# A chunked delta-rule recurrence: products with the same shape of stationary tile issued directly together

## The chip, the core and the metric

The kernel runs on one core of a Trainium2 chip. The metric is the device time in microseconds (us) of one execution. TensorE (PE in the profile) does matrix products, VectorE (DVE) and ScalarE (ACT) elementwise work, GpSimd (POOL) a few powers and fills, and the SyncE queue (SP) issues the transfers.

## The reference, cut to what matters

Two layers of a decoder trunk on 256 tokens of width 2048, float32. Layer 0 runs an RG-LRU and an mLSTM side by side. Layer 1, where the change lies, is an RWKV-7 time mixing: 64 heads of 64 features, and for each head a state matrix that is updated token by token.

```python
def step(S, inp):
    r_t, w_t, k_t, v_t, kk_t, a_t = inp
    sa = jnp.einsum('bhvk,bhk->bhv', S, -kk_t)
    S = (S * w_t[:, :, None, :] + sa[..., None] * (kk_t * a_t)[:, :, None, :]
         + v_t[..., None] * k_t[:, :, None, :])
    return S, jnp.einsum('bhvk,bhk->bhv', S, r_t)
...
u = h @ w_in                       # 2048 x 16384: r, k, v and the gate z
...
y = head_norm(y.reshape(B, S, RWKV_WIDTH), H, RWKV_GN_EPS, gn_g, gn_b)
bonus = jnp.sum(rh * kh * r_k.astype(jnp.float32), axis=-1, keepdims=True) * vh
...
return (y * jax.nn.silu(z)) @ w_out
```

## The kernel before, in words

Most of the time goes to four big projections (in and out of each layer). Their weights are loaded in pieces (`raw`), and each piece is split into a high part (`whi`, copied by ACT) and the rest (`wlo`, subtracted by DVE), so that three products replace one float32 product: `hh` and `hl` (high part and rest of the activations) with `whi`, then `hh` with `wlo`. These products write banks named `gb`. A piece of an input projection is 16 products with `whi` and 8 with `wlo`.

Everything else (the mixers) writes banks named `mb` and is woven between those products. A mixer is a Python generator; a `yield w` says how much projection work should come before its next step. `Weave` counts the projection work as it is written out (`tick`, 0.44 for four products) and lets a generator go on when its due time has come; after a step that issued TensorE work it lets at least 0.4 pass. TensorE runs strictly in the order in which it was written (`InOrder`). On DVE and ACT the framework orders the instructions itself, except that none passes a split of the weights that was written before it (`Behind`); the order is fixed when the program is built.

Layer 1 works through eight groups of eight heads (`g` = 0 to 7). A group needs four input projections of 512 columns (k, r, z, v). The recurrence of group g, `recur`, starts when its v is there, and so runs between the products of the k projection of group g+1 (for g = 7 between those of the output projection). It goes over four chunks of 64 tokens. For each chunk `c` there are up to five sets of eight small products (four pairs of heads, two heads each); the letters are used below:

- W: `mb<-UV,At`, all chunks; ACT copies the result to `Ws`;
- U: `mb<-Ws,TT`, all chunks; DVE multiplies the result by `Gn` into `UV`, one half of the partitions at a time;
- S: `mb<-UV,BKt`, chunks 0 to 2, the new state; DVE adds the old state and multiplies by the decay (`Sn<-Sn,mb`, then `Sn<-Sn,PC`), and ACT copies the result in two halves to the next chunk's `UV` (`UV<-Sn`), which the next W reads;
- A: `mb<-UV,At` again, all chunks, the outputs from the current chunk, into the banks `Yb`;
- R: `mb<-Sn,Rc`, chunks 1 to 3, the outputs from the old state, into the same banks.

S and A have stationary tiles of 128 rows by 64 columns; U and R of 64 by 64. Each set stands by itself between projection products. After chunk 1 and after chunk 3 `norm` takes the two banks `Yb`: three copies `Yn<-mb` and a square on ACT, a sum over each head on DVE (`TENSOR_REDUCE vr`), a small `TENSOR_SCALAR vr`, a power on POOL (`vr<-vr,mhalf`), and the product `Yn<-Yn,vr` on DVE, which waits for that power.

At the same time `keys` of group g+1 runs in another lane: when the k projection ends, `kt` and `sq` are made, TensorE sums squares (`mb<-cs,sq`), DVE reads the sums (four `Gn<-mb`), multiplies `kP<-kt,th`, and then makes the eight parts of `BK` from `xx` and `zz`, which ACT makes.

Of the kernel before, what the change touches and what calls it, by code (L numbers as in the profile page):

```python
# [13 lines left out]
P = 128  # L14
# [12 lines left out]
# columns of the packed per-feature vectors: (name, tiles)  # L27
# [18 lines left out]
# columns of the constant array  # L46
# [10 lines left out]
class Weave:  # L57
    """Steps of the mixers, emitted between the products of the projections. A step yields the amount of
    products that come before its lane goes on."""
# [41 lines left out]
class InOrder:  # L101
    """The tensor engine, issuing in the order of the program."""
# [19 lines left out]
class Behind:  # L122
    """An engine whose instructions follow, in its own order, the splits of the weights emitted before them."""
# [20 lines left out]
def two_layers(ctx, tc, x, gpost, cst, selc, v0, v1, w_in0, w_out0, w_in1, w_out1, lruw, qkvw,  # L144
# [36 lines left out]
    def keep_warm(n, b):  # L181
        """Products that keep the clock of the tensor engine up while it waits; nothing reads them."""
        for _ in range(n):
            pe.matmul(b, lhsT=ones[:, 0:P], rhs=ones, start=True, stop=True)
# [15 lines left out]
    # ---------------------------------------------------------------- products  # L200
    def split_w(raw, w=512, into=None):
        """Weights to their high part and the rest."""
# [17 lines left out]
    def in_mms(banks, hi, lo, pc, h, nft, tick):  # L220
        """One piece (two k-tiles) of an input projection: first what needs the high parts of the weights alone."""
# [17 lines left out]
    def in_proj(wsrc, h):  # L239
        """512 columns of an input projection, features on partitions: two banks of two tiles."""  # L240
        banks = [gbank(), gbank()]
        for pc in range(8):
            in_mms(banks, *split_w(load_w(wsrc[pc])), pc, h, 4, 0.44)
        return banks
# [10 lines left out]
    def out_proj(wsrc, get_y, evac, tick, finish, after, room=None):  # L255
        """Output projection, tokens on partitions; get_y(g): the two parts of k-tiles 4g..4g+3. The last
        pieces of the last chunk go token tile by token tile, so that what follows the first is covered."""
# [49 lines left out]
    # ---------------------------------------------------------------- norms, tokens on partitions  # L307
    def rstd(ss):
        """ss [P, 4]: partial sums of squares of a token tile -> [P, 1]."""
# [10 lines left out]
    def scale(ss, pool_):  # L320
        """diag(rstd) of a token tile: transposes by products with it are scaled."""
# [4 lines left out]
    def to_features(xs, dg, g, warm):  # L326
        """Four tiles [P, 2, 512] of tokens, scaled by dg and g, to the two parts of h."""
        banks = {}
# [34 lines left out]
    def log1p_of(e, tmp):  # L363
        """log(1 + e), 0 <= e <= 1, as 2 atanh(e / (2 + e)); tmp: three tiles like e."""
# [12 lines left out]
    def silu2(banks, sz):  # L377
        """sz = 2 silu of two banks."""
# [6 lines left out]
    def residual(layer, tile_of):  # L385
        """The evacuation of out_proj: sums of squares, and the products with the post-norm's weights."""
# [17 lines left out]
    # ================================================================ layer 0  # L404
    with ExitStack() as l0:
# [35 lines left out]
        # small tables  # L441
# [37 lines left out]
        # ------------------------------------------------------------ mLSTM inputs  # L479
# [6 lines left out]
        def mlstm_in(c, xm):  # L486
# [43 lines left out]
            # both gates: two column tiles side by side, summed at the end  # L530
# [104 lines left out]
        # ------------------------------------------------------------ RG-LRU  # L635
# [70 lines left out]
        def room():  # L706
            """Parts of the weights in the place of what the heads have done with."""
# [18 lines left out]
    # ================================================================ layer 1  # L726
    with ExitStack() as l1:
# [19 lines left out]
        # derived per-feature vectors; the halves of the heads' partitions swap B and K  # L747
# [19 lines left out]
        def loras():  # L767
            """The first halves of the two loras: the token shift is taken after the product."""
# [35 lines left out]
        def decay(g, st):  # L804
            """What depends on the loras: the decay within chunks of 64 tokens, and the rate."""
# [481 lines left out]
```

## Time and profile before

| | |
|---|---|
| median of 3 runs | 1917.44 us (1916.8 to 1917.52) |
| profiled execution: span from the first to the last instruction | 1912.7 us |
| median less span: what lies around the span | 4.7 us |
| mean granted TensorE clock | 0.997 |
| PE busy, share of the span | 98% |
| DVE busy | 73% |
| ACT busy | 55% |

Busy times are of instructions from start to end; TensorE's instructions overlap, so that the step from one start to the next is what one costs, and not its duration. A line of the groups or of the timeline gives the engine, the line of the code, the operation, what it writes and reads, the shape, and its time. All matmuls of the kernel have line L116 and all DVE and ACT instructions L132, since helpers record them, so names of tiles tell them apart. A float32 product of the mixers leaves two records in the trace (x16 for a set of eight), a projection product one.

### The profile page before, as it was taken

To read this page: it belongs to the slowest core of one execution; us is meant where nothing else is said; L and a number is where in the kernel's file an instruction comes from. 1 tells how busy PE (TensorE), PEld (TensorE's weight loads), DVE (VectorE), ACT (ScalarE), POOL (GpSimd) and SP (SyncE) were. 2 spreads that over 40 slices of the span, in tenths; PEclk is the share of its full clock that TensorE was granted. 3 is DMA by queue.
4 is the path that set the end of the run, shared out by engine and by line. 5 is a ranking of instruction groups with operands and counts; after the bars stand their busy time and mean duration, and the time that the engine had idled before them with its cause. 6 is when DMAs were issued, how large, how long until landed. Compare 5 with 4: busy or idle time off the path is not lost.

```text
span 1912.7 us, 39517 instructions
## 1 busy us (share of the span) xinstructions
PE 1883.4 (98%) x16498; PEld 1747.9 (91%) x16498; DVE 1395.3 (73%) x2302; ACT 1044.1 (55%) x1609; POOL 60.4 (3%) x84
## 2 busy tenths in 40 slices
PE   8999999999999999999999999999999999999998
PEld 7999999999888899989999999999999999997886
DVE  5667777757554569969689689597796896895544
ACT  5444666645444546555565555655655655555442
POOL 0000000000000100000000000000000000000000
PEclk9999999999999999999999999999999999999999
DMA  7433545455666444434444434344344443356664
GB/s 250 142 133 111 177 162 169 155 171 194 215 208 195 168 147 135 152 118 144 133 136 138 133 130 155 111 147 149 113 150 139 136 136 131 122 187 203 211 202 156
DMA packets 86947, 299.63 MB, mean 157 GB/s; under 512 B 9576, under 2 KB 12392, under 8 KB 86768
## 3 DMA queue, kind: packets, MB, share of 16 engines
q1 hardware_dynamic: 86768, 297.11, 47.2%
q8 instruction: 129, 2.11, 0.5%
q14 instruction: 50, 0.41, 0.1%
HBM read 289.20 MB, written 7.86 MB: 155 GB/s over the span
## 4 chain that ended last, share of the span: by engine, by line
PE 93%; DVE 4%; ACT 1%; issue 1%; DMA 0%; POOL 0%; SPq 0%; DVEq 0%; POOLq 0%; ACTq 0%
PE gb L116 75%; PE mb L116 17%; DVE wlo L132 2%; PE mb L119 1%; DVE wb L132 1%; ACT whi L132 1%; DMA xq<-in_x_dram 0%; DVE rt L132 0%; DVE Tb L132 0%; DVE tf L132 0%; DVE Ab L132 0%; DVE yT L132 0%; ACT ZT L132 0%; ACT vt L132 0%; DVE At L132 0%
## 5 line engine op out<-in xcount | busy, mean ns | idle before, releaser
L132 DVE TENSOR_TENSOR wlo<-raw,whi 128x1024 fp32r<-128x1024 f32 x509 | 619.9, 1219 | 338.0 <-ACT whi L132 304.5
L132 ACT CAST whi<-raw 128x1024 fp32r<-128x1024 f32 x509 | 532.6, 1048 | 557.3 <-PE gb L116 512.3
L116 PE MATMUL gb<-hh,whi 128*128 128x256 f32 x3120 | 790.5, 289 | 2.8 <-ACT whi L132 2.8
L116 PE MATMUL gb<-hl,whi 128*128 128x256 f32 x3120 | 770.6, 283 | 0.0
L116 PEld LDWEIGHTS gb<-hh,whi 128*128 128x128 f32 x3120 | 596.7, 191 | 13.6 <-ACT whi L132 3.7
L116 PEld LDWEIGHTS gb<-hl,whi 128*128 128x128 f32 x3120 | 597.5, 192 | 0.8
L116 PE MATMUL gb<-hh,wlo 128*128 128x256 f32 x3120 | 453.5, 286 | 0.0
L116 PEld LDWEIGHTS gb<-hh,wlo 128*128 128x128 f32 x3120 | 404.9, 191 | 4.2 <-issue 0.7
L116 PE MATMUL gb<-whi,yl 128*128 128x512 f32 x500 | 136.9, 392 | 0.5 <-DVE yl L132 0.5
L116 PE MATMUL gb<-whi,yh 128*128 128x512 f32 x500 | 136.5, 392 | 0.0
L116 PE MATMUL gb<-wlo,yh 128*128 128x512 f32 x500 | 135.7, 390 | 0.0
L116 PEld LDWEIGHTS gb<-whi,yl 128*128 128x128 f32 x500 | 93.2, 188 | 20.4 <-DVE yl L132 0.9
L116 PEld LDWEIGHTS gb<-wlo,yh 128*128 128x128 f32 x500 | 93.5, 188 | 19.8
L116 PEld LDWEIGHTS gb<-whi,yh 128*128 128x128 f32 x500 | 93.0, 188 | 19.3
L132 DVE TENSOR_TENSOR Tb<-Tb,tf 64x31 f32<-64x31 f32 (+15 forms) x248 | 82.6, 333 | 6.1
L132 DVE TENSOR_TENSOR tf<-Ab,Tb 64x31 f32<-64x31 f32 (+15 forms) x248 | 81.9, 330 | 4.5
L116 PE MATMUL mb<-AR,BK 64*128 64x128 f32 (+1 forms) x1024 | 58.0, 253 | 7.0 <-DVE AR L132 6.0
L116 PEld LDWEIGHTS mb<-AR,BK 64*128 64x128 f32 (+1 forms) x1024 | 50.2, 161 | 13.3 <-PE gb L116 7.1
L132 DVE TENSOR_TENSOR UV<-mb,Gn 64x256 f32<-64x256 f32 x64 | 26.9, 421 | 34.5 <-PE mb L116 33.4
L132 ACT ACTIVATE zz<-kP,dv 128x256 f32<-128x256 f32 x64 | 32.3, 505 | 22.9 <-DVE kP L132 12.4
L116 PEld LDWEIGHTS mb<-UV,At 128*64 128x64 f32 (+1 forms) x1024 | 35.0, 137 | 10.3 <-issue 2.5
L1125 POOL TENSOR_TENSOR vr<-vr,mhalf 128x8 f32<-128x8 f32 x16 | 28.3, 1771 | 499.4 <-DVE vr L132 499.4
(258 smaller groups left out, 1855.9 us busy)
## 6 DMA issues: line engine op xcount, KB each, us to landing
raw<-in_w_in_dram SPq DMA_DIRECT2D x384, 512.0 KB, 3.3
raw<-in_w_out_dram SPq DMA_DIRECT2D x128, 512.0 KB, 4.3
y1d<-zt SPq DMA_DIRECT2D x7, 512.0 KB, 3.9
yraw<-y1d SPq DMA_DIRECT2D x7, 512.0 KB, 4.3
l<-in_lora_dram SPq DMA_DIRECT2D x8, 384.0 KB, 4.6
xq<-in_x_dram SPq DMA_DIRECT2D x8, 256.0 KB, 5.2
lw<-in_lruw_dram SPq DMA_DIRECT2D x4, 512.0 KB, 4.6
xr<-in_x_dram SPq DMA_DIRECT2D x8, 256.0 KB, 6.0
```

What stands on the lines that cost most here:

```text
L116: return self._chain(self.eng.matmul(*a, **k))
L119: return self._chain(self.eng.transpose(**k))
L132: r = op(*a, **k)
L1125: pool.tensor_tensor(vr, vr, mhalf[:, 0:8], ALU.pow)
```

## The change

In `recur`, R moves up from the end of its chunk to directly behind U of the same chunk, and opens the accumulation in `Yb`; A moves up to directly behind S and ends it. The two banks `Yb` of chunks 0 and 2 are therefore taken before S and not after it. The two `yield`s behind A and R (0.2 and 0.25) are gone, so that the next chunk's W is due 2.4 after S. The step in which chunk 1 hands its banks to `norm` now comes after that 2.4. Nothing is computed differently, apart from the order of the two terms in the sum. (Comments are gone too; they shift nothing.)

```diff
                 ub = mbank()
...
+                if c % 2 == 0:
+                    Yb = [mbank(), mbank()]
+                cr = [slice(64 * ((c + hd) % 2), 64 * ((c + hd) % 2) + 64) for hd in range(2)]
+                if c:
+                    for f in range(4):
+                        for hd in range(2):
+                            hr = slice(64 * hd, 64 * hd + 64)
+                            pe.matmul(Yb[hd][cr[hd], f * 64:(f + 1) * 64], lhsT=Rc[hr, f, c, :],
+                                      rhs=St[hr, f, :], start=(f == 0), stop=False, skip_group_check=True)
                 for hd in range(2):
                     hr = slice(64 * hd, 64 * hd + 64)
                     dve.tensor_tensor(UV[hr, c, :, hd, :], ub[hr, 0:256].rearrange("p (f v) -> p f v", f=4),
                                       Gn[hr, :, c:c + 1].broadcast_to([64, 4, 64]), MUL)
                 yield 1.8
-                Sp = St
                 if c < 3:
                     sb = mbank()
...
+
+                for f in range(4):
+                    for hd in range(2):
+                        pe.matmul(Yb[hd][cr[hd], f * 64:(f + 1) * 64], lhsT=At[:, f, hd, c, 64:128],
+                                  rhs=UV[:, c, f, hd, :], start=(c == 0 and f == 0),
+                                  stop=True, skip_group_check=True)
+                if c < 3:
                     Sn = g1.tile([P, 4, 64], F32, name="Sn", tag="Sn", bufs=2)
...
                     St = Sn
                     yield 2.4
-                # outputs of this chunk
-                if c % 2 == 0:
-                    Yb = [mbank(), mbank()]
-                cr = [slice(64 * ((c + hd) % 2), 64 * ((c + hd) % 2) + 64) for hd in range(2)]
-                for f in range(4):
-                    for hd in range(2):
-                        pe.matmul(Yb[hd][cr[hd], f * 64:(f + 1) * 64], lhsT=At[:, f, hd, c, 64:128],
-                                  rhs=UV[:, c, f, hd, :], start=(f == 0),
-                                  stop=(c == 0), skip_group_check=True)
-                yield 0.2
-                if c:
-                    for f in range(4):
-                        for hd in range(2):
-                            hr = slice(64 * hd, 64 * hd + 64)
-                            pe.matmul(Yb[hd][cr[hd], f * 64:(f + 1) * 64], lhsT=Rc[hr, f, c, :],
-                                      rhs=Sp[hr, f, :], start=False, stop=True, skip_group_check=True)
-                    yield 0.25
                 if c == 1:
                     nm = wv_.add(norm(0, Yb, Yn, Yn[:, 1]), 2)
```

On TensorE, in chunk 2 of group 3's recurrence, the end of the chunk read as follows before: A, R, and the W of chunk 3, each between projection products.

```order
L116 MATMUL mb<-UV,At 64x64 x8
L116 MATMUL gb<-hh,wlo 128x256 x4
L116 MATMUL mb<-Sn,Rc 64x64 x8
L116 MATMUL gb<-hh,wlo 128x256 x4
L116 MATMUL mb<-UV,At 64x64 x8
```

After the change, U and R of the same chunk stand together, then four projection products and the sums of squares of the next group's keys.

```order
L116 MATMUL gb<-hh,wlo 128x256 x4
L116 MATMUL mb<-Ws,TT 64x64 x8
L116 MATMUL mb<-Sn,Rc 64x64 x8
L116 MATMUL gb<-hh,wlo 128x256 x4
L116 MATMUL mb<-cs,sq 128x2 x8
```

Twelve projection products later S and A stand together, and the W of chunk 3 follows 20 projection products behind them; before, from S to that W, there were 24 projection products, A, 4, R, and 4 more. Over the whole program the stretches of mixer products between projection products go from 307 to 259. The sums of squares stood between the W and the U of chunk 2 before, 16 projection products and U ahead of S; now U and R are past, and 12 projection products lie between the sums and S.

On DVE, the same place read as follows before, from the reading of the sums to the product with the power (names in brackets are the engines waited for):

```order
L132 TENSOR_SCALAR Gn<-mb 64x8 x3
L132 TENSOR_TENSOR kP<-kt,th 128x1024
L132 RECIPROCAL Gn<-Gn 128x16 [waits DVE_49]
L132 TENSOR_TENSOR UV<-mb,Gn 64x4x64 [waits PE_49]
L132 TENSOR_TENSOR UV<-mb,Gn 64x4x64
L132 TENSOR_TENSOR BK<-xx,zz 128x4x64 [waits Activation_49]
L132 TENSOR_REDUCE vr<-Yn 128x8
L132 TENSOR_TENSOR Sn<-Sn,mb 128x256 [waits PE_49]
L132 TENSOR_SCALAR vr<-vr 128x8 [waits DVE_49]
L132 TENSOR_TENSOR Sn<-Sn,PC 128x256 [waits DVE_49]
L132 TENSOR_TENSOR wlo<-raw,whi 128x1024 [waits DMAHW1_49,PE_49,Activation_49]
```

And as follows after the change, in groups 1 to 6 alike:

```order
L132 TENSOR_SCALAR Gn<-mb 64x8 x3
L132 TENSOR_TENSOR kP<-kt,th 128x1024
L132 RECIPROCAL Gn<-Gn 128x16 [waits DVE_49]
L132 TENSOR_REDUCE vr<-Yn 128x8
L132 TENSOR_TENSOR BK<-xx,zz 128x4x64 [waits Activation_49]
L132 TENSOR_SCALAR vr<-vr 128x8 [waits DVE_49]
L132 TENSOR_TENSOR Sn<-Sn,mb 128x256 [waits PE_49]
L132 TENSOR_TENSOR Yn<-Yn,vr 128x512 [waits Pool_49]
L132 TENSOR_TENSOR wlo<-raw,whi 128x1024 [waits DMAHW1_49,PE_49,Activation_49]
L132 TENSOR_TENSOR BK<-xx,zz 128x4x64 [waits Activation_49]
L132 TENSOR_TENSOR Sn<-Sn,PC 128x256 [waits DVE_49]
```

The second product of the state (`Sn<-Sn,PC`) stood two places behind the first; now the product that waits for the power, a split of weights and a part of `BK` stand between them.

## The prediction

> **What bounds the kernel now.** I read the page's parts 1 and 4 first, then who waits for whom on TensorE, and then the timeline of one recurrence (group 1, from 940 to 976 us).
>
> ```profile
> PE 1883.4 (98%) x16498; PEld 1747.9 (91%) x16498; DVE 1395.3 (73%) x2302; ACT 1044.1 (55%) x1609; POOL 60.4 (3%) x84
> PE 93%; DVE 4%; ACT 1%; issue 1%; DMA 0%; POOL 0%; SPq 0%; DVEq 0%; POOLq 0%; ACTq 0%
> ```
>
> TensorE has work at all times, and the chain that ended last is TensorE's own order. So whatever shortens TensorE's list of work, or makes it wait, moves the end by as much. The waits (engine, tile, releaser; us in total, times, longest) are few:
>
> ```profile
> PE mb L116 <- DVE dg L132: 6.2, 3, 3.6
> PE mb L116 <- DVE AR L132: 6.0, 6, 1.0
> ```
>
> No wait for `UV` or `Sn` is among the long ones. The price of a set is in the steps of the timeline (start, us, engine):
>
> ```profile
> 949.12 0.28 PE L116 MATMUL gb<-hl,whi 128*128 128x256 f32 x1
> 949.33 0.69 PE L116 MATMUL mb<-UV,At 128*64 128x64 f32 x16
> 949.94 0.39 PE L116 MATMUL gb<-hh,whi 128*128 128x256 f32 x1
> 950.16 0.28 PE L116 MATMUL gb<-hl,whi 128*128 128x256 f32 x1
> 950.28 0.28 PE L116 MATMUL gb<-hh,whi 128*128 128x256 f32 x1
> 950.62 0.69 PE L116 MATMUL mb<-UV,At 128*64 128x64 f32 x16
> ```
>
> A projection product steps 0.12 us (950.16 to 950.28). From 949.12 to 950.16 there are two such steps (0.24) and a set, so the set costs 1.04 - 0.24 = 0.80. A longer stretch of one kind, 32 products, tells how much of this is the products:
>
> ```profile
> 845.09 0.28 PE L116 MATMUL gb<-hl,whi 128*128 128x256 f32 x1
> 845.29 2.08 PE L116 MATMUL mb<-AR,BK 64*64 64x64 f32 x64
> 847.30 0.74 PE L116 MATMUL gb<-hh,wlo 128*128 128x256 f32 x4
> ```
>
> Here 845.09 to 847.30 is 2.21, against 0.82 (949.12 to 949.94) for 8: the 24 further products take 1.39, 0.058 each. Eight take 0.46, so 0.80 - 0.46 = 0.34 of a set is paid for leaving the projection's shape and coming back.
>
> **The merged sets: -16.3 us, and +0.7 back.** Before, a group has 18 such stretches (4 sets in chunk 0, 5 in chunks 1 and 2, 4 in chunk 3); now 12. Over 8 groups 48 go, 48 x 0.34 = 16.3 us, all on TensorE, with nothing beside them. That two sets of one shape join at no cost is not shown. From below it costs nothing, as inside the 32 products; from above it costs the whole 0.34. It is nearest to the 32 products, which change bank in the middle. In 24 joints (odd chunks) two neighbours use the same column half, so that one step may be lost; half of 24 x 0.058 is +0.7.
>
> **A wait that goes: -2.5 us.** Chunk 2's S waits for `UV` today:
>
> ```profile
> 967.41 0.28 PE L116 MATMUL gb<-hl,whi 128*128 128x256 f32 x1
> 967.62 1.04 PE L116 MATMUL mb<-UV,BKt 128*64 128x64 f32 x16
> 968.59 1.22 PE L116 MATMUL gb<-hh,wlo 128*128 128x256 f32 x8
> ```
>
> From start to the next projection product it takes 0.97, the set above 0.61: 0.36 of waiting, at this place in groups 0 to 6, 7 x 0.36 = 2.5. With R behind U and U earlier, `UV` is done before S comes.
>
> **A wait that comes: +22.8 us.** W of the next chunk waits for the state's chain: S, two DVE products, two ACT copies. Before, A, R and 32 projection products covered it; now A and 20 to 24. In chunks 0 and 1 that is enough. For chunk 2 of groups 1 to 6 the built order puts `Yn<-Yn,vr` (behind POOL's power), a split and a `BK` between the two DVE products, and all of it behind `kP`, which waits for the sums of squares. These rows price it (they stand in the old order):
>
> ```profile
> 964.73 0.36 PE L116 MATMUL gb<-hh,whi 128*128 128x256 f32 x1
> 965.37 0.44 PE L116 MATMUL mb<-Ws,TT 64*64 64x64 f32 x7
> 964.90 0.70 DVE L132 TENSOR_SCALAR Gn<-mb 64x8 f32<-64x8 f32 x4 [0.40 <-PE mb L116]
> 965.63 1.23 DVE L132 TENSOR_TENSOR kP<-kt,th 128x1024 f32<-128x1024 f32 x1
> 966.77 0.25 DVE L132 RECIPROCAL Gn<-Gn 128x16 f32<-128x16 f32 x1
> 967.05 0.88 DVE L132 TENSOR_TENSOR UV<-mb,Gn 64x256 f32<-64x256 f32 x2
> 967.96 0.43 DVE L132 TENSOR_TENSOR BK<-xx,zz 128x256 f32<-128x256 f32 x1
> 968.30 0.68 DVE L132 TENSOR_REDUCE vr<-Yn 128x8 f32<-128x512 f32 x1
> 969.01 0.42 DVE L132 TENSOR_TENSOR Sn<-Sn,mb 128x256 f32<-128x256 f32 x1
> 969.35 0.17 DVE L132 TENSOR_SCALAR vr<-vr 128x8 f32<-128x8 f32 x1
> 969.60 1.80 POOL L1125 TENSOR_TENSOR vr<-vr,mhalf 128x8 f32<-128x8 f32 x1 [48.00 <-DVE vr L132]
> 969.47 0.42 DVE L132 TENSOR_TENSOR Sn<-Sn,PC 128x256 f32<-128x256 f32 x1
> 970.07 0.82 ACT L132 COPY UV<-Sn 64x256 f32<-64x256 f32 x2
> 969.90 1.23 DVE L132 TENSOR_TENSOR wlo<-raw,whi 128x1024 fp32r<-128x1024 f32 x1
> 971.04 0.42 DVE L132 TENSOR_TENSOR BK<-xx,zz 128x256 f32<-128x256 f32 x1
> 971.43 0.69 DVE L132 TENSOR_TENSOR Yn<-Yn,vr 128x512 f32<-128x512 f32 x1
> 972.04 0.42 DVE L132 TENSOR_TENSOR BK<-xx,zz 128x256 f32<-128x256 f32 x1
> ```
>
> Count from the first `Gn` (964.90), start to start, in the new order. DVE: `Gn` 0.73, `kP` 1.14, reciprocal 0.28, reduce 0.71, `BK` 0.34: the small `vr` starts at 3.20. POOL starts 0.25 after that (969.35 to 969.60) and takes 1.80: 5.25, and `Yn` follows within 0.03. `Yn` 0.61, split 1.14, `BK` 0.39: `Sn<-Sn,PC` starts at 7.42 and ends at 7.84, and the copies end 0.82 later, at 8.7. TensorE: the projection resumes behind the sums of squares at 964.73, 0.17 before the count; four products and the change of shape take 0.64 (to 965.37), eight more 0.96, so S starts at 1.43. S and A take 0.61 + 0.46 = 1.07. The 20 products take 0.68 for the first four (949.94 to 950.62) and 16 x 0.12: W stands ready at 5.1. It waits 8.7 - 5.1 = 3.6. The part of the count that could shrink is the start, and that is later rather than earlier: `kt`, a split and an `AR` now stand ahead of `Gn` too, and I find DVE up to 0.4 late. I take 3.8, six times: 22.8. Behind W the whole projection waits, since TensorE runs in order. The ends: 2.7 if the split could run ahead of the power (3.8 less 1.14), 5 if DVE is later by another 1.2, one more split.
>
> Group 0 has a transposition between the two products, and group 7 (chunk 1) the copies of `norm` and a split on ACT ahead of the copies of the state:
>
> ```profile
> 988.27 2.01 DVE L132 STREAM_TRANSPOSE Ab<-Aab 32x1024 f32<-32x1024 f32 x1
> 963.47 1.14 ACT L132 COPY Yn<-mb 128x256 f32<-128x256 f32 x3
> ```
>
> By the same count the first costs about 0.8 (0.7 from S to its result, 0.4 + 2.0 + 0.4 + 0.8 against W at 3.7), and the second, with 0.2 in chunk 2, another 0.8: +1.6.
>
> **The clock: +6 us.** TensorE waits of some us are rare here. Two of them, with the stretches of 3.41 us around them (PE busy, ..., granted clock):
>
> ```profile
> 9.64 0.60 PE L116 MATMUL mb<-dg,xq 128*128 128x128 f32 x3 [3.60 <-DVE dg L132]
> 651.38 0.82 PE L116 MATMUL mb<-dg,xr 128*128 128x128 f32 x5 [1.91 <-DVE dg L132]
> 7.73:11.15 3.42, 1.51 (x13) 1.51 (x14) 0.45 (x2) 2.56 (x9) 0.75 (x2) 1.00 1.01 349
> 649.43:652.85 3.42, 1.51 (x14) 1.47 (x14) 2.52 (x4) 0.97 (x3) 1.49 (x2) 1.00 0.84 231
> 652.85:656.26 3.41, 3.41 (x19) 3.41 (x18) 3.29 (x9) 3.14 (x9) 0.00 (x0) 0.50 0.67 244
> ```
>
> After 1.91 of waiting the clock fell to half for 3.41 us; after 3.60 it did not. In such a stretch 19 products ran where 0.12 steps make 28, a loss of 9 x 0.12 = 1.1. A wait of 3.8 is nearer to both than to none. I take 1.0 each, 6 in all; the ends are 0 and 2 x 1.7 x 6 = 20, two stretches at half clock each time.
>
> The Trainium skill (TensorE: Matmul & The Clock Gate, section "Why this matters for your kernels") warns against gaps of over some 3 us between bursts, since one idle window brings half clock. By that rule all six waits bring a stretch, about 1.7 each, and the sum would be 4 us higher. The trace does not agree with it as a bound: 1.91 was enough once and 3.60 was not.
>
> **The sum.** -16.3 + 0.7 - 2.5 + 22.8 + 1.6 + 6.0 = +12.3 us, on a span of 1912.7 and 4.7 around it, which is the median of the runs (1917.4). I forecast 1930.
>
> **The rivals.**
> - *The state's chain is not late (faster).* W of chunk 3 finds its data, because the chain in front of it is shorter on the chip than the sum of its steps. For it: before, no such wait exists. Against it: POOL's 1.80 and the split stand between two products of one queue. The gain decides while the wait stays under (16.3 - 0.7 + 2.5 - 1.6) / 6 = 2.75 us with the clock full, 1.75 with the clock's 1.0. With no wait at all in groups 0 to 7: 1917.4 - 18.1 = 1899.
> - *The wait comes, the clock stays full.* As after the 3.60 wait: 1930 - 6 = 1924.
> - *Two stretches of half clock each, or DVE later.* 1930 + 6 x 2.4 = 1944.
> - *The joint is not free:* the change of tiles inside a stretch costs what leaving it cost; the change does not do what it says. Against it stand the 32 products in 2.21. 1930 + 15.6 = 1946.
>
> **How the numbers follow.** Chances: the forecast 0.55, full clock 0.17, no or short wait 0.15, the two costly ones 0.13 together. A difference of under 0.2% (3.8 us) is about what cannot be told from no change. The forecast's own range is 1922 to 1938, the costly cases lie above 1921 as well, and of the full-clock case three quarters: slower 0.78. Of the short waits most are faster: 0.13. The rest, 0.09, is the same. The range for 8 in 10 leaves out most of the no-wait case and the top of the costly ones: 1910 to 1943.
>
> **What would show it.** Sets of 16 and 16 records with one gap around them, 0.46 apart; 259 stretches. In groups 1 to 6, W of chunk 3 waiting 3 to 4.5 us for ACT's `UV<-Sn`, at the head of TensorE's waits with some 20 to 27 us in total; `Yn<-Yn,vr` on DVE right behind POOL, and `Sn<-Sn,PC` after it; a few stretches at clock 0.50 after those waits. I am wrong if the waits by `UV<-Sn` sum to under 10 us, or the joints show more than 0.1 us.

## The result, and the profile after

The change makes the kernel slower: 1952.13 us median of 4 runs (1950.9 to 1952.5) against 1917.48 us (4 runs) on the same chip, a ratio of 1.0179 with a 95% interval of 1.0165 to 1.0192. The forecast was 1930 with a range up to 1943: the direction was right, the size was not. The medians differ by 34.7 us. The profiled execution spans 1950.6 us, 37.9 more than before. The two figures differ because the profiled execution of the kernel before was one of its shortest: in every run on record the time is 1.7 to 1.9 us above the span, so a span of 1912.7 belongs to a time of 1914.5 and not to the median, and the 4.7 us given above as what lies around the span are mostly that difference.

Parts 1 and 4 of the page after: busy time of TensorE has hardly moved, but the chain that ended last now is something else than TensorE's own work for 18% of the span (7% before).

```profile
PE 1890.2 (97%) x16498; PEld 1763.5 (90%) x16498; DVE 1396.6 (72%) x2302; ACT 1044.0 (54%) x1609; POOL 59.7 (3%) x84
PE 82%; DVE 9%; ACT 4%; issue 2%; POOL 1%; DMA 0%; SPq 0%; DVEq 0%; POOLq 0%; ACTq 0%
```

TensorE's waits after (what it waits for; us in total, times, longest). The first row was foreseen, the growth of the second from 6.0 us was not, nor the third, a single wait at 880 us.

```profile
PE mb L116 <- ACT UV L132: 19.9, 10, 3.3
PE mb L116 <- DVE AR L132: 12.8, 6, 2.3
PE mb L119 <- DVE Yn L132: 3.4, 1, 3.4
```

The merged sets do what was forecast. TensorE's timeline after, S and A in group 1:

```profile
961.27 0.28 PE L116 MATMUL gb<-hl,whi 128*128 128x256 f32 x1
961.48 0.69 PE L116 MATMUL mb<-UV,BKt 128*64 128x64 f32 x16
962.00 0.64 PE L116 MATMUL mb<-UV,At 128*64 128x64 f32 x16
962.56 0.39 PE L116 MATMUL gb<-hh,whi 128*128 128x256 f32 x1
962.78 0.28 PE L116 MATMUL gb<-hl,whi 128*128 128x256 f32 x1
```

From 961.27 to 962.78 are 1.51, less two steps of 0.12: 1.27 for both, where two single sets cost 0.80 each. The joint costs nothing; the second set starts 0.52 behind the first. U and R step 1.27 in even chunks and 1.10 in odd ones (medians, single sets 0.80 and 0.81). Over 24 joints of S and A, and of U and R 8 in even chunks and 16 in odd ones, TensorE's list is 8.1 + 2.7 + 8.2 = 19.0 us shorter.

A large part of what ate this up is seen at the W of chunk 3, here in group 1, on DVE, ACT and TensorE (the bracket: idle time before, and who ended it):

```profile
984.52 0.42 DVE L132 TENSOR_TENSOR Sn<-Sn,mb 128x256 f32<-128x256 f32 x1
986.25 0.69 DVE L132 TENSOR_TENSOR Yn<-Yn,vr 128x512 f32<-128x512 f32 x1 [1.31 <-POOL vr L1124]
986.86 1.22 DVE L132 TENSOR_TENSOR wlo<-raw,whi 128x1024 fp32r<-128x1024 f32 x1
988.00 0.42 DVE L132 TENSOR_TENSOR BK<-xx,zz 128x256 f32<-128x256 f32 x1
988.33 0.42 DVE L132 TENSOR_TENSOR Sn<-Sn,PC 128x256 f32<-128x256 f32 x1
988.86 0.81 ACT L132 COPY UV<-Sn 64x256 f32<-64x256 f32 x2
989.30 1.11 PE L116 MATMUL mb<-UV,At 128*64 128x64 f32 x16 [1.79 <-ACT UV L132]
```

Between the state's two products on DVE lie 3.8 us, 1.31 of them idle for POOL. The same thing happens later with the second norm, between two parts of `Aab`, and delays the `AR` for which the scores' products wait:

```profile
1001.08 0.69 DVE L132 TENSOR_TENSOR Aab<-mb,Gn 64x512 f32<-64x512 f32 x1
1002.87 0.69 DVE L132 TENSOR_TENSOR Yn<-Yn,vr 128x512 f32<-128x512 f32 x1 [1.09 <-POOL vr L1124]
1018.91 1.91 PE L116 MATMUL mb<-AR,BK 64*128 64x128 f32 x16 [2.26 <-DVE AR L132]
```

In the kernel before, this product came after all four parts of `Aab` and a split, and POOL was done by then; the wait for AR was 1.0 us.

The larger surprise is the clock. After the change 18 stretches show a granted clock of 0.50 (20 windows of 3.41 us, the one at the very end left out), against 2 before. Two of the 20 lie at 8.8 us, ahead of everything that the change moved. The count also differs between executions of one kernel: most executions of the kernel before have a mean clock of 0.994 to 0.996, the profiled one has 0.997, and one window lowers it by about 0.0009 (half of 3.41 us in 1950), so that by this estimate an ordinary execution of it has one to three windows more. Summed over TensorE's steps (each against the median of the same step undisturbed), the two executions differ by -19.0 (sets), -2.5 (the wait of S, by the prediction's price; the steps show 2.6), +34.9 (waits, 17.8 to 52.7) and +24.0 (half clock, 0.8 to 24.8): +37.4, against 37.9 measured.

By place, 19.6 us of it lie in the five rounds from the sums of squares of group 2's keys to those of group 7's, and 14.1 in the one round before them (from 827 to 979 us, 152.0 instead of 137.9), where the rest of group 0's recurrence runs: a W waits 2.3 us there, `norm`'s transposition 3.4, the inverse of group 1 1.6, and five half-clock windows fall into it.

### The profile page after: what moved, and what is told of

Same layout as the page of the kernel before. It is cut to its first block, busy times and chain, and to the rows that moved or that the text cites. A ratio compares the mean times of both kernels' runs of the same rounds, so it can differ in the third digit from the quotient of the medians.

```text
span 1950.6 us, 39522 instructions
## 1 busy us (share of the span) xinstructions
PE 1890.2 (97%) x16498; PEld 1763.5 (90%) x16498; DVE 1396.6 (72%) x2302; ACT 1044.0 (54%) x1609; POOL 59.7 (3%) x84
## 4 chain that ended last, share of the span: by engine, by line
PE 82%; DVE 9%; ACT 4%; issue 2%; POOL 1%; DMA 0%; SPq 0%; DVEq 0%; POOLq 0%; ACTq 0%
PE gb L116 67%; PE mb L116 14%; DVE wlo L132 3%; ACT whi L132 1%; PE mb L119 1%; POOL vr L1124 1%; DVE Ab L132 1%; DVE Aab L132 1%; ACT Yn L132 1%; ACT UV L132 0%; ACT kt L132 0%; DVE vr L132 0%; DVE zt L132 0%; DVE BK L132 0%; DVE kP L132 0%
## 5 line engine op out<-in xcount | busy, mean ns | idle before, releaser
L116 PE MATMUL gb<-hh,wlo 128*128 128x256 f32 x3120 | 460.1, 289 | 0.0
L116 PEld LDWEIGHTS gb<-hh,wlo 128*128 128x128 f32 x3120 | 413.8, 195 | 3.1 <-issue 0.7
L116 PE MATMUL mb<-AR,BK 64*128 64x128 f32 (+1 forms) x1024 | 56.9, 258 | 13.8 <-DVE AR L132 12.8
L116 PE MATMUL mb<-UV,At 128*64 128x64 f32 (+1 forms) x1024 | 47.2, 230 | 20.8 <-ACT UV L132 19.9
L116 PEld LDWEIGHTS mb<-AR,BK 64*128 64x128 f32 (+1 forms) x1024 | 49.1, 165 | 19.8 <-issue 13.9
L132 DVE TENSOR_TENSOR UV<-mb,Gn 64x256 f32<-64x256 f32 x64 | 26.9, 421 | 25.7 <-PE mb L116 24.8
```

The costliest lines, as they stand in the source:

```text
L116: return self._chain(self.eng.matmul(*a, **k))
L132: r = op(*a, **k)
```

## The experiments

Medians in us, with the ratio to the kernel before on the same chip and its 95% interval. Half-clock windows are counted without the end of the run; waits are TensorE's, summed over all rows. Both are those of the one profiled execution, which need not be the median one (e2: 1932.5, e3: 1950.2).

| run | us | ratio | waits | half-clock windows |
|---|---|---|---|---|
| before | 1917.5 | | 21.3 | 2 |
| after | 1952.1 | 1.0179 (1.0165 to 1.0192) | 51.6 | 20 |
| e1_hold | 1955.5 | 1.0195 (1.0172 to 1.0217) | 54.6 | 17 |
| e2_warm | 1938.0 | 1.0093 (1.0073 to 1.0113) | 31.7 | 4 |
| e3_late | 1947.0 | 1.0151 (1.0134 to 1.0168) | 51.8 | 18 |
| e5_sar | 1946.1 | 1.0143 (1.0127 to 1.0158) | 39.2 | 20 |
| e6_normpool | 1937.2 | 1.0101 (1.0083 to 1.0119) | 47.4 | 12 |
| e7_allpool | 1967.5 | 1.0252 (1.0235 to 1.0270) | 65.4 | 25 |
| e8_before_allpool | 1954.1 | 1.0183 (1.0168 to 1.0198) | 48.3 | 15 |
| e9_late_allpool | 1954.3 | 1.0188 (1.0173 to 1.0203) | 54.3 | 15 |
| e11_sar_due | 1937.2 | 1.0094 (1.0079 to 1.0109) | 40.1 | 10 |
| e12_ar_due | 1940.2 | 1.0117 (1.0094 to 1.0140) | 39.1 | 14 |
| e13_late_due | 1926.6 | 1.0038 (1.0025 to 1.0050) | 42.3 | 11 |
| e14_before_due | 1928.6 | 1.0051 (1.0035 to 1.0068) | 19.8 | 6 |
| e15_nopow | 1922.7 | 1.0029 (1.0017 to 1.0040) | 36.4 | 10 |
| e16_early | 1953.3 | 1.0188 (1.0174 to 1.0202) | 32.7 | 16 |
| e17_tuned | 1910.3 | 0.9963 (0.9949 to 0.9976) | 24.0 | 6 |
| e21_apart_due | 1938.1 | 1.0107 (1.0092 to 1.0121) | 32.4 | 3 |
| e22_apart_tuned | 1921.1 | 1.0013 (1.0004 to 1.0022) | 17.9 | 7 |
| e23_tuned2 | 1908.4 | 0.9946 (0.9934 to 0.9959) | 25.5 | 4 |

**Is POOL's power in DVE's queue the cause?** e15 keeps the order of DVE around the state and takes only the wait for POOL away (the kernel then leaves the normalisation out):

```diff
-            dve.tensor_tensor(yo, yo, vr.unsqueeze(2)...
+            dve.tensor_tensor(yo, yo, mhalf[:, 0:8].unsqueeze(2)...
```

> The changed kernel, in which norm's product on DVE multiplies by a constant tile in place of POOL's power (the normalisation of the heads is left out; the power is still computed and read by nobody). The order of DVE's instructions around the state is the same; only the wait for POOL inside DVE's queue, 1.1 to 1.3 us each time, is gone, and no work moves to POOL. Theory 1: W's waits of 1.9 to 3.3 us fall by 1.3 each (22.7 us to about 14), those for AR from 2.2 to 1.1 (13.8 to 7), and 8 to 12 of 19 half-clock stretches go: 1918 to 1930. If the power were not the cause, the waits stay and the time is 1948 or more. If waits fall but the clock does not recover: 1935 to 1940.

DVE at the same place as above:

```profile
975.66 0.42 DVE L132 TENSOR_TENSOR Sn<-Sn,mb 128x256 f32<-128x256 f32 x1
976.00 0.69 DVE L132 TENSOR_TENSOR Yn<-Yn,mhalf 128x512 f32<-128x512 f32 x1
976.60 1.22 DVE L132 TENSOR_TENSOR wlo<-raw,whi 128x1024 fp32r<-128x1024 f32 x1
977.74 0.42 DVE L132 TENSOR_TENSOR BK<-xx,zz 128x256 f32<-128x256 f32 x1
978.08 0.42 DVE L132 TENSOR_TENSOR Sn<-Sn,PC 128x256 f32<-128x256 f32 x1
```

TensorE's first two waits:

```profile
PE mb L116 <- ACT UV L132: 13.3, 10, 1.9
PE mb L116 <- DVE AR L132: 6.8, 6, 1.2
```

The two products of the state are 2.42 apart instead of 3.81. Waits for UV and AR fall by 6.6 and 6.0, 10 half-clock windows of 20 go, and the time falls by 29 us. So in the changed kernel DVE's waits for a power of 1.7 us on POOL are worth, with the clock they cost, 29 of the 35 us lost: shown by the run. The same edit was not run on the kernel before; there DVE hardly waits for the power, as its rows say (before, then after):

```profile
DVE Yn L132 <- POOL vr L1125: 3.0, 2, 1.8
DVE Yn L132 <- POOL vr L1124: 21.0, 16, 1.8
```

The power alone is not the whole cause: without it 13.3 us of waits for UV stay, and in e17 below, the merged sets at other due times, DVE waits 23.0 us for it and the kernel is faster than before. Such a wait costs time where TensorE's list no longer covers it.

**Is the half clock a consequence of waits?** e2 puts work where TensorE waited:

```diff
                 wb = mbank()
+                if c == 3 and g < NG - 1:
+                    keep_warm(14, wb)
```

> The changed kernel with 14 added products of 128x512 (about 3.1 us, into a bank that nothing reads) ahead of the W of chunk 3 in groups 0 to 6, where TensorE waits 1.9 to 3.3 us. Theory 1 (an idle stretch brings the half clock): the waits for UV<-Sn turn into work of the same length, so the time falls only by the half-clock stretches behind them, 5 to 7 of some 19, by 6 to 10 us, to 1942 to 1946; the stretches behind the AR waits stay. Theory 2 (dense small products bring the half clock): the stretches stay, time 1950 to 1954.

The waits for UV fell to 2.0 and the time by 14, more than forecast: besides the windows behind W, those behind AR went too (4 left of 20), though TensorE still waited 1.7 us there. (The profiled execution, 1932.5 us, is the shortest of four; by their mean clock of 0.992 to 0.993, against its 0.995, the others had an estimated two or three windows more.) The length of one wait does not decide it, then. The tables of windows show what does (stretch; its length; busy time and records of TensorE, of its weight loads and of the other engines; clock; share and rate of the transfers). Each second row is the window that follows. The changed kernel:

```profile
1121.47:1124.88 3.41, 0.89 (x16) 0.73 (x16) 2.29 (x5) 1.79 (x5) 0.00 (x0) 1.00 0.31 111
1124.88:1128.30 3.42, 3.42 (x19) 3.38 (x16) 0.42 (x1) 2.42 (x6) 0.00 (x0) 0.51 0.12 48
988.35:991.76 3.41, 2.36 (x28) 2.16 (x29) 1.25 (x4) 3.12 (x8) 0.00 (x0) 1.00 0.43 154
991.76:995.18 3.42, 3.42 (x54) 3.22 (x53) 2.45 (x5) 2.70 (x5) 0.94 (x1) 1.00 0.11 20
```

The run e5, at the sums of squares of group 2:

```profile
970.79:974.20 3.41, 2.53 (x32) 2.29 (x28) 3.30 (x7) 2.67 (x6) 0.00 (x0) 1.00 0.40 137
974.20:977.62 3.42, 3.38 (x16) 3.38 (x16) 2.96 (x9) 0.46 (x2) 0.00 (x0) 0.53 0.43 153
```

The run e2, at a wait for AR:

```profile
1008.34:1011.75 3.41, 1.70 (x16) 1.52 (x14) 3.34 (x10) 0.97 (x3) 0.00 (x0) 1.00 0.71 232
1011.75:1015.17 3.42, 3.42 (x36) 3.30 (x37) 3.42 (x10) 1.15 (x2) 0.13 (x1) 1.00 0.63 214
```

A window with 0.89 us of work is followed by half clock, one with 2.36 is not. But in e5 2.53 us of busy time was not enough, in e2 1.70 was: the window of e5 held 4 projection products (256 columns each) and small ones with 2 or 64 columns, that of e2 14 projection products. I counted the moving columns of each window of 3.413 us that ran at full clock, over all 20 traces (a window full of projection products has some 7,200):

```text
columns in the window   windows   followed by half clock
under 1500                   57       57
1500 to 2999                158      101
3000 to 4499                484       36
4500 and more             10270        0
```

So it goes by the columns streamed in a fixed window: of those with under 3000, two fifths of a full one, 158 of 215 were followed by half clock, of the others 36 of 10,754, and idle time and narrow products take columns away alike. Busy time separates worse: 75 of the 194 windows that half clock followed were busy for 2.4 us or more. A wait of 2 us costs a half-clock window (1.2 us, 24.8 over 20) if it falls into one window together with small sets, and may cost nothing if the window's border cuts it, as at 988.35 in the third row, where the wait ran from 987.5 to 989.3. Shown by count; only e2 changed the streamed work on purpose. The Trainium skill (TensorE: Matmul & The Clock Gate, section "What's actually happening") describes a free-running window of 3413 ns, which agrees; its advice in "Why this matters for your kernels", to avoid idle gaps of more than some 3 us, does not go far enough here, where waits of 1.9 us and a window with no single wait above 0.6 us brought the half clock.

**Is it the earlier W, or the merging?** e3 merges with W later, e16 moves W earlier with the sets apart:

```diff
 e3: the changed kernel           e16: the kernel before
-                    yield 2.4   -                    yield 2.4
+                    yield 4.2   +                    yield 1.0
```

> The changed kernel with 4.2 in place of 2.4 as the yield behind the state: sets merged as in the change (258 stretches against 259), but W of the next chunk some 16 projection products later, as far from S as before the change or farther, and the two products of the state adjacent on DVE. Theory 1 (merging pays what the joints show, about 18 to 20 us, and all of the loss is the earlier W and what follows from it): no wait for UV<-Sn over 0.5, time 1898 to 1912, faster than the kernel before; what is left of the waits for AR decides where in that range. Theory 2 (merged sets themselves bring the half clock): 1915 to 1930 with 10 or more half-clock stretches and no long waits ahead of them.

> The kernel before with the yield behind the state 1.0 in place of 2.4: the next W 12 to 14 projection products earlier, as the change does, but all sets apart. If the early W does the harm: waits for UV<-Sn of 12 us or more appear, with half-clock stretches behind them, 1935 to 1955. If merging does the harm: under 4 us of such waits, 1914 to 1922.

Both are slow, and neither fits one theory. e3 has no wait of W for the state any more, as its first theory said, but takes 1947.0 us where at most 1912 was expected. e16's time lies in the range for the early W, but not its waits. TensorE's first two waits in e3:

```profile
PE mb L116 <- DVE AR L132: 18.5, 6, 3.1
PE mb L116 <- ACT sq L132: 11.4, 8, 1.7
```

And in e16:

```profile
PE mb L116 <- DVE BK L132: 12.2, 13, 1.0
PE mb L116 <- ACT sq L132: 5.8, 14, 0.8
```

No wait for ACT's `UV` is left in e3, and only 1.4 us in e16, where 12 or more were expected. So W is just one place of several. DVE and ACT have a fixed list of work from the end of the k projection to AR (`sq`, `Gn`, `kP`, `BK`, `Aab`, transpositions, `AR`), and TensorE's list beside it is its cover. The due times count projection products only; the sets between them are cover that nobody counts. Between the sums of squares and the 32 products with BK, the built order has 80 projection products before and after, but 8 sets in 8 stretches before, and 6 sets in 4 stretches after: 80 x 0.12 + 8 x 0.80 = 16.0 us against 9.6 + 1.27 + 0.80 + 1.10 + 0.80 = 13.6. The cover is 2.4 us a group shorter, and the engine that is late next shows it: W here, BK, sq or AR elsewhere. Of the 2.4 only 0.83 comes from the two joints (0.33 and 0.50); 1.6 are U and R of chunk 2, which now stand ahead of the sums of squares. A set that moves past such a place takes cover away as one that gets cheaper does.

**Taking the delay out of the queue.** e1 pins the state's products and copies ahead of everything written later; e6 moves the product with the power to POOL; e7, e8 and e9 move more to POOL.

```diff
 e1: +  act.hold = dve.hold = True     (around the products of the state and the copies to UV)
 e6: -  dve.tensor_tensor(yo, yo, vr...    +  pool.tensor_tensor(yo, yo, vr...
 e7 to e9, besides: yT<-yT,vt and zt<-zt,yT on pool (groups 0 to 6)
```

> The changed kernel, but nothing that is written later gets ahead of the state's two products on DVE and of the two copies to UV on ACT; TensorE's order is that of the changed kernel (259 stretches). Theory 1 (the product that waits for the power, the split and BK between the two products make W late, and each such wait also brings a stretch at half clock): the waits of TensorE for UV<-Sn, 19.9 us and more, fall to under 3, about 6 of some 19 half-clock stretches go (1.4 us each), and the time falls by 28 to 34, to 1918 to 1924. The waits for AR (12.8 us) and their half-clock stretches stay. Theory 2 (the half clock comes from the small products standing densely together, not from waits): the waits go, the number of half-clock stretches stays near 19, time 1930. Theory 3 (W is late for another reason, such as POOL or the sums of squares): under 5 us change.

> The changed kernel with one instruction moved: the product of norm that waits for POOL's power (Yn<-Yn,vr, 128x512, 0.69 us on DVE) runs on POOL behind the power, so that it stands in no queue ahead of the state, of Aab or of AR. Theory 1 (the wait for the power inside DVE's queue makes both W and AR late): of DVE's 1.3 us idle and 0.6 for the product ahead of the second state product, and as much ahead of AR, both go: the waits for UV<-Sn fall from 22.7 to 6 to 10 us, those for AR from 13.8 to 3 to 6, and about half of the 19 half-clock stretches (1.4 us each) go with them: 1914 to 1926. Theory 2 (DVE is simply full from the keys to AR, and the order inside does not matter): only the 0.6 us of each product is gained, the waits fall by 16 x 0.6 at most: 1940 to 1948. Theory 3 (POOL's 128x512 product slows DVE, or is late for the transposition that reads it): 1950 or more.

> The run before with two more steps of the group that ends moved from DVE to POOL: the sum yT<-yT,vt and the product with the gate zt (its factor 0.5 as an instruction of its own), 2.6 us of DVE per group that stand ahead of AR. If DVE's fullness ahead of AR makes the waits for AR, they fall under 3 us in total and the half-clock stretches behind them go: 6 to 14 us faster than the run before. If not, it is equal to it within 4 us.

> The kernel before with the same three steps on POOL, as a control: what POOL's help is worth without the change. By theory 1 only its six waits for AR (6.8 us in all, 1.07 each) go: 1910 to 1914. If POOL's work slows DVE or holds a transfer back: 1917 or more.

> The merged sets with the later W (4.2 in place of 2.4) and the three steps on POOL. The merged sets gain some 20 us against the control if nothing waits. Theory 1: no W wait, the 22 us of waits for AR (3.15 each) fall by half or more, and the low windows behind them with the half-clock stretches: 1896 to 1912, faster than the control. Theory 2 (merged small sets take so many columns out of a window of 3.4 us that the clock halves with no wait at all): 10 or more half-clock stretches stay, 1915 to 1930.

e1 took away W's waits (2.7 us of step excess left of 22.7) and gained nothing: with the copies pinned on ACT, splits and `Ws` came late (13.6 us of waits for `whi`, 11.0 for `Ws`). e6 landed between the theories, with 16.2 us of waits for UV and 9.4 for AR left. e7, e8 and e9 missed altogether, e8 by 40 us, and the control says why. DVE in e8, and POOL beside it:

```profile
1003.91 0.22 DVE L132 TENSOR_TENSOR Tb<-Tb,tf 64x60 f32<-64x60 f32 x1
1004.72 1.36 DVE L132 TENSOR_TENSOR tf<-Ab,Tb 64x112 f32<-64x112 f32 x1
1006.12 1.33 DVE L132 TENSOR_TENSOR Tb<-Tb,tf 64x112 f32<-64x112 f32 x1
...
1004.67 1.29 POOL L1108 TENSOR_TENSOR yT<-yT,vt 128x512 f32<-128x512 f32 x1
1006.03 1.29 POOL L1137 TENSOR_TENSOR zt<-zt,yT 128x512 f32<-128x512 f32 x1
```

A DVE product of 64x112, 0.27 us elsewhere, takes 1.36, from POOL's start to POOL's end: a two-operand product on POOL stops one on DVE that starts behind it until it ends. The other way round POOL waits: a `zt<-zt,yT` that started 0.2 us behind a split on DVE took 2.17 us instead of 1.29. So much of POOL's 11 us a group (two of each, 1.05, 1.48, 1.36 and 1.71 us) was no relief but an addition, and AR came up to 4.6 us late. In e6 the `BK` behind the state takes 1.27 instead of 0.42 for the same reason. The Trainium skill (SBUF — State Buffer, section "Who interferes with whom") says that a VectorE instruction with two inputs in SBUF and a GpSimd one that reads it lock each other out. The rows agree for POOL's two-operand products; beside POOL's scaling of `zt`, which reads SBUF as well, most of DVE's products kept their usual pace (0.22 at 1003.91).

**Does a change of shape inside a stretch cost?** e5 puts R behind A, so that tiles of 64x64 follow tiles of 128x64.

> The changed kernel with R moved from behind U to behind A, so that S, A and R stand together (stationary tiles 128x64, 128x64, then 64x64): again 259 stretches, but one joint per chunk 1 and 2 where the shape changes, and in chunk 3 A and R together. If only leaving the projection's shape costs (0.34 us), the shape of the neighbour does not matter: S, A and R step about 1.73 us together (0.805 + 0.46 + 0.46) and the time is within 4 us of the changed kernel's 1952. If a change of shape between two small sets costs what leaving costs, they step about 2.07, and the 24 joints cost 8 us more: 1958 to 1962. The waits of W stay in both.

Outside half-clock stretches S, A and R step 1.89 us (8 of 14), 0.62 more than S and A; the set's own products are 0.46. A and R in chunk 3 step 1.48, 0.67 more than one set. A joint with a change of shape costs 0.16 to 0.21 us, more than nothing and less than the 0.34 of leaving and coming back. The time fell by 6 nevertheless, since W comes later there and its waits are gone (14.6 us for AR and 6.5 for sq remain).

**Giving the covers back by due times.** In e11 (order of e5), e12 (the changed kernel), e13 (e3) and e14 (the kernel before) the products that wait are made due later:

```diff
 in scores, ahead of the products with AR (e11 to e14):   -  yield 2     +  yield 4.5
 in keys, ahead of the sums of squares (e11; e13):        -  yield 2.4   +  yield 3.6; 4.2
```

> The order S, A, R (the run e5) with two due times moved: the yield ahead of the scores' products with AR 4.5 in place of 2, so that these come 24 projection products later, and that ahead of the sums of squares 3.6 in place of 2.4 (12 products later). No work is changed or taken off an engine. Theory 1 (the merged sets shortened TensorE's list between the k projection's end and AR, DVE's list there did not get shorter, and TensorE now waits for it; each wait of 2 us and more also brings a half-clock stretch): the waits for AR, 14.6 us, fall under 4, those for sq, 6.5, under 3, and of 17 half-clock stretches of e5 6 at most stay: 1908 to 1922. Theory 2 (dense small sets alone halve the clock): 10 or more stay, 1924 to 1935.

> The changed kernel with the scores' products with AR alone 24 projection products later (4.5 in place of 2). The waits of W stay. Theory 1: waits for AR 12.8 us to under 3, and the six half-clock stretches behind them go (1.4 us each): 1930 to 1937. If the clock has nothing to do with these waits: 1940 to 1944. If they return at the next place where TensorE needs DVE: 1948 or more.

> The merged sets with the later W (the run e3) and both due times moved (4.5 in place of 2 ahead of AR, 4.2 in place of 2.4 ahead of the sums of squares). Theory 1: the waits for AR (18.5 us) and sq (11.4) fall under 6 together and most half-clock stretches go: 1900 to 1918, the fastest so far. Theory 2: the stretches stay at 10 or more, 1922 to 1932.

> The kernel before with AR alone 24 products later, as a control: its six waits for AR (1.0 each) go and nothing else changes: 1910 to 1914. What the merged sets are worth is then measured against this.

The waits that were aimed at went, but all four came out slower than first expected, the control by 14 us; e12's 1940.2 lies in the range that was given for a clock that these waits do not touch, though its half-clock windows fell from 20 to 14. In e11 later sums of squares made `BK` late (22.0 us). In e14 the waits for AR went, and as much came back in other places: by the steps, waits of 17.8 became 22.3 and the half clock's 0.8 became 8.8, and it is 9.4 us behind the kernel before. What sets its windows is open. e13 was nearest. Its time and its 11 half-clock windows are what the theory of the dense small sets named, but 25.1 us of waits at two new places are left, so that it decides nothing about that theory. Its rows name them in group 2:

```profile
1128.40 1.15 PE L116 MATMUL mb<-AR,BK 64*64 64x64 f32 x32 [1.15 <-DVE UV L132]
1140.91 0.63 PE L119 MATMUL mb<-cs,Yn 128*128 128x128 f32 x4 [2.28 <-DVE tf L132]
```

e17 makes these two due later as well, and e21 and e22 are e13 and e17 with the sets apart (W due 3.75 behind S, plus the 0.2 and 0.25 behind A and R, in place of 4.2):

```diff
 e17 = e13 and:  keys, group 0 only:                -  yield 4.2    +  yield 2.4
                 blocks, ahead of the products:     -  yield 3.5    +  yield 4.8
                 the second norm, at its end:       -  yield 0.68   +  yield 3.0
                 scores:                            -  yield 4.5    +  yield 2.4
```

> The run e13 (merged sets, later W, AR and sums of squares) with three more due times moved: the first group's sums of squares as before the change, the products with BK 1.3 later, the transpositions of the second norm 2.3 later (AR as much less, so that it stays where it was). If the waits that e13 showed for BK (2.5 us a group) and ahead of the transpositions (1.5) are only late DVE work, they fall by two thirds: 1908 to 1920. If TensorE then waits for the same DVE work at the next place: within 4 us of e13's 1926.6.

> The run e13 with the sets apart, as in the kernel before: the same due times of W, AR and the sums of squares counted in projection products, 307 stretches in place of 259. The difference to e13 is what merging alone is worth. If the joints pay as the trace shows (0.34 us each, 48 of them): 16 us slower than e13 if neither waits, about 1940. If DVE sets the pace there and TensorE waits out what it saves: within 5 us of e13's 1926.6.

> The run e17 with the sets apart (307 stretches): the same due times counted in projection products. If a joint saves 0.34 us and nothing waits in either, 16 us slower than e17's 1910.3: 1922 to 1930. If the sets apart cover waits that e17 still has, 8 to 12 us slower: 1917 to 1922. If the due times alone make e17 fast: within 4 us of 1910.

> The run e17 with the second norm's later transpositions only in groups 1 to 6, and as before the change in groups 0 and 7. In e17 TensorE waits 2.7 us at 889 us for BKt, behind ACT's wait for the transfer that frees zt, with two half-clock windows behind it. If that follows from the later norm of group 0: this wait and its windows (1.4 us each) go, 1904 to 1908. If not: 1909 to 1912.

TensorE's waits in e17, where the long rows of the changed kernel are gone:

```profile
PE mb L116 <- DVE dg L132: 4.0, 2, 2.1
PE gb L116 <- ACT whi L132: 2.8, 4, 0.9
PE mb L119 <- DVE tf L132: 2.7, 6, 0.8
PE mb L116 <- ACT BKt L132: 2.7, 1, 2.7
```

e17 is faster than the kernel before, and e22 says what merging alone does there: 1921.1 - 1910.3 = 10.8 us (e21 against e13: 11.5), of the 19.0 by which TensorE's list is shorter. These pairs ran on different chips; by their ratios to the kernel before on the same chip it is 0.50% or 9.6 us (e21 against e13: 0.69% or 13.2), and the two traces of e22 and e17 differ by 9.5. The rest returns as waits: from e22 to e17 the 28 scores' stretches take 2.9 us more in all, the 16 transpositions 3.8 and the 8 stretches with 32 products 2.0, which is 8.7 of the missing 9.5. With 6 half-clock windows in e17 and 7 in e22, merged sets alone do not halve the clock. From one group's sums of squares to the next's it is 129.7 us in e17, 130.3 in e22, 131.1 in the kernel before and 134.6 to 136.0 in the changed one. e23 takes the late norm out of groups 0 and 7. Its gain is below the expected one: the wait for `BKt` went, but one of 2.1 for `At` took its place with the same two half-clock windows. At 1908.4 it is the fastest version, 0.5% under the kernel before.

## Why the prediction was right or wrong

- *The merged sets, -16.3 and +0.7 back:* right in mechanism, low in size. The joint is free, as the 32 products said. The +0.7 was of the wrong sign: in odd chunks records of U and R alternate, and the pair steps 1.10, not 1.27. Measured 19.0.
- *The wait of S that goes, -2.5:* gone, as forecast; the steps at that place were 1.17 us in groups 1 to 6 and 1.26 in group 0, against 0.81 undisturbed, 2.6 in all; after the change S and A step 1.27 there wherever the clock is full.
- *W behind the state, +22.8 and +1.6:* right. 24.4 forecast, 19.9 in the waits' row, 22.7 as excess of the steps; the rows named (power, split, `BK`) stand between the two products. Groups 1 to 6 waited 1.8 to 3.3 instead of 3.8: 3.25 in four of them, and 1.8 in groups 1 and 4, where a half-clock stretch just ahead of W (at 981.6 and 1387.8) brought TensorE to it later.
- *The clock, +6: the step that failed.* Measured 24.0. The argument took two waits and the clock after each, and priced a wait by its length, 1.0 each at six places. What counts is the columns streamed in a window of 3.41 us, small sets included; 18 more windows were hit, also at AR, at the small sets ahead of W and in group 0 (two of them at 8.8 us, where the change has no part). The upper end of 20 was passed. Groups 1 to 6 do show the two stretches each that it assumed, but one of them lies at AR and not at W.
- *What was missing, the second step that failed:* waits other than W's, put at nothing, measured +12.2 as excess of the steps, 7.0 of them for AR (6.8 to 13.8) and 3.4 for group 0's norm. I followed the state's chain alone and did not ask what else the shorter list of TensorE had covered. The row of waits for AR, 6 times 1.0, was quoted as a small wait; it said that DVE set the pace there, so that time taken from TensorE ahead of it could come back. Group 0 was priced at 0.8 us; its round grew by 14.1.
- *The rivals:* "two stretches each, or DVE later" (1944) was nearest, and given too little of the chance. A full clock and a free W were wrong. The joint is not dear.

Of the 25.6 us between the forecast +12.3 and the +37.9 between the profiled executions (34.7 between the medians), the clock is 18.0 and the missed waits 12.2; W and the sets came out 1.7 and 3.4 better than forecast, which leaves 0.5.

## What to carry to other kernels

Work taken off the busiest engine is only a gain where no other engine's list ends just behind it; a row of equal short waits, one a group, marks a place where a saving can come back as a wait. Where due times count only part of the work, merging or moving the uncounted part shifts everything that was tuned to it, so tune the due times again before judging the merge (here +1.8% became -0.4%). And price a wait on TensorE with its window: what counts is whether enough columns are streamed beside it.

## What the runs showed of the hardware that was not expected

- The clock halves for 3.41 us after a window with few columns: always under 1500 of some 7,200 (57 of 57), never from 4500 up (0 of 10,270), whether the rest is idle or narrow products. In between it was 137 of 642.
- Two sets of 64x64 tiles interleave where the second takes the other half of the columns: U and R step 1.10 us in odd chunks, against 1.27 in even ones, where they take the same half. A joint with a change from 128x64 to 64x64 costs 0.16 to 0.21.
- A two-operand product on POOL stretched a two-operand product on DVE from 0.27 to 1.36 us, and was stretched itself from 1.29 to 2.17 behind a split on DVE: the later one waits. While POOL scaled `zt` (1003.16 to 1004.70), three of the four DVE products that started took their usual 0.22 to 0.24 us and one 0.48.
